# A two-layer four-group mixer on one core: gated outputs of groups C and B wait in DRAM, group D's second keys are made ahead of B's gate, and the ordering clock charges other instructions

## The chip, the cores and the metric

One core of one Trainium2 chip runs the whole program in one launch. The metric is the device time of an execution in microseconds (us). TensorE is called PE, VectorE DVE, ScalarE ACT, GpSimd POOL and SyncE SP, as in the profile; PEld is TensorE's weight load.

## What is computed

Two layers (`DEPTH = 2`), each on 1024 tokens of width 1024, float32. Cut to what matters here:

```python
h = rmsnorm(x, g_pre) @ w_in            # one projection of 3488 columns
ya = swa_sink_attention(a_q, a_k, a_v)  # A: window 128, 4 heads, sinks
yb = short_gated_conv(b_b, b_c, b_x)    # B: b * conv3(c * x)
yc = mla(c_q, c_kv, c_kr)               # C: causal softmax attention, 4 heads
yd = stick_breaking_attention(d_q, d_k, d_v)   # D: 4 heads
y  = rmsnorm(stack([ya, yb, yc, yd])) * silu(gate)   # norm per group of 256
x  = x + rmsnorm(y @ w_out, g_post)
```

Group D's weights for one query block: `a = exp(log_sigmoid(z) + after)`, `after` being a reversed cumulative sum of `log_sigmoid(-z)` over the keys.

## The kernel before

**Precision and tiles.** Every matmul works on operands split into a high and a low part (two reduced-precision tiles per float32 tile), so a projection is three matmuls per 128 rows of the contraction: 24 matmuls for 128 output columns by 512 tokens. One `g` tile holds 128 partitions by 1024 float32 values; the pool `gp` has 34 of them, and they hold the split input (16 tiles, `xt`), queries, keys, values and the groups' outputs `L["y"]` (two tiles a group, one for each half Q of the tokens). Weights come by DMA into two `raw` buffers, are split by ACT (high part) and by POOL or DVE (low part) into three `W` tiles, and from there feed PE.

**The weave.** The program is not written in the order of execution. The class `Weaver` (from line 96) keeps a clock of its own for ACT, DVE, POOL and the DMA queue, and `run` chooses, step by step, among generator functions ("streams"): the first stream in the list whose next operands are there by that clock goes next on PE, or else the one that is ready soonest. The order so found is fixed on every engine (`behind`, `in_order`); at run time each engine takes its instructions in that order and waits where an operand is late. `enter` (from line 255) gives each instruction a duration from its shape; `half` adds 125 ns on ACT and 95 ns on DVE for an output of at most 64 partitions; `pair` keeps DVE and POOL instructions apart that would start inside one another.

**The streams that matter.** `gemm()` (line 1639) issues the projections: C, B, D's values, `d_q(0)`, `d_k(0)`, the gate of group C (`gate(L, 2)`), `d_q(1)`, then half of the gate of group B, then `d_k(1)` (the keys of D's heads 2 and 3), which waits for D's first scores (`need(("scores", l, "D0"))`), then B's other half, A's values and queries, and, after `("scores", l, "D1")`, A's keys. `scores()` issues the score matmuls of C, D heads 0 and 1 (D0), D heads 2 and 3 (D1) and A; it comes ahead of `gemm()` in the list, so projections fill PE where no scores are ready. `pvs()` transposes the weights and multiplies by the values. For D each query block needs, on DVE, a scan and a product over up to 1024 columns. `norms()` normalises each group; B's output has waited in DRAM (`yBd`) since the convolution and is loaded into `g` tiles once `("D", l, 0)` is marked. `z_parts()` splits the gated outputs C, B, D (`z_split`, line 1505) for the output projection after A's scores; `w_out_rows()` loads and splits the output weights; `outs()` does the output projection, eight token tiles by two halves. All DMAs are issued by SP, in one order.

**The tight pool.** When `d_q(1)` is done, the 34 `g` tiles are all taken: 16 of `xt`, 2 each of the outputs B, C and D, 4 of D's values, 6 of D0's queries and keys, 2 of D1's queries. D1's keys need 4 (`room(4)` in `d_k`).

Of the kernel before, what the change touches and what calls it, by code (L numbers as in the profile page):

```python
# [21 lines left out]
P = 128  # L22
# [71 lines left out]
class Weaver:  # L94
# [7 lines left out]
    def __init__(self, tc):  # L102
        self.tc = tc
        self.now = 0.0
        self.busy = {k: [] for k in "AVGDH"}
        self.acc = {}
        self.touched = {}
        self.opened = {}
        self.slots = {}
        self.banks = set()  # L110
        self.read = {}
        self.table = None
        self.users = []
        self.load_at = 0.0
        self.start = 0.0
        self.gone = set()
        self.last, self.tag = {}, {}
        self.funcs = [(0.0, 0)]
        self.port = {"V": [], "G": []}
        self.done = set()  # L120

    def alloc(self, ap, tag, bufs):
# [43 lines left out]
    def after(self, key, a, kinds):  # L166

        p0, p1, lo, hi = self.area(a)
        name = a.tensor.name
        t = self.opened.get(name, 0.0)  # L170
        if name not in self.acc:
            t = max(t, self.last.get(self.tag.get(name), 0.0))
        for (q0, q1, l, h, kind, k), end in self.acc.get(name, {}).items():
            if kind in kinds and q0 < p1 and p0 < q1 and l < hi and lo < h:
                t = max(t, end + LAT.get(k + key, 0.0))
        return t

    def ready(self, key, aps):
        return max([self.after(key, a, "w") for a in aps], default=0.0)
# [68 lines left out]
    def enter(self, key, op, args, kw):  # L248
        aps = [a for a in list(args) + list(kw.values()) if isinstance(a, bass.AP)]
        out = aps[0]  # L250
        outs = [out]
        if "accum_out" in kw:
            outs.append(kw["accum_out"])
        if op == "tensor_tensor_reduce":
            outs.append(aps[-1])
        n = 1
        for d in (aps[1] if op == "tensor_reduce" else out).shape[1:]:
            n *= d
        t = max(self.ready(key, aps[1:]), max(self.after(key, a, "rw") for a in outs))
        read = [a.tensor.name for a in aps[1:] if a.tensor.name in self.banks]  # L260
        bank = bool(read)
        for nm in read:
            for k, end in self.read.get(nm, {}).items():
                t = max(t, end + (LAT[k + key] if k != key else 0.0))
        scalars = sum(
            isinstance(args[i], bass.AP) for i in SCALARS.get(op, ()) if i < len(args)
        )
        func = args[2] if op == "activation" else None
        pair = False
        half = out.shape[0] <= 64 and n >= 128  # L270
        if key == "A":
            dur = (52.0 if bank else 93.0) + 0.833 * n
            dur += 93.5 * sum(isinstance(kw.get(k), bass.AP) for k in ("scale", "bias", "accum_out"))
            dur += 125.0 * half
            if func in TABLES and func:
                t = max(t, self.load_at)
        elif key == "V":
            fast = op == "tensor_scalar" and not bank
            dur = 69.0 + (0.52 if fast else 1.04) * n + 62.0 * scalars + 95.0 * half
            pair = (fast or op == "tensor_tensor") and not bank and n >= 128  # L280
            if op == "tensor_tensor_scan":
                dur = 110.0 + 2.12 * n
                pair = True
            elif op == "tensor_reduce":
                dur += 117.0
        elif op == "affine_select":
            dur = 244.0
        elif op == "memset":
            dur = 36.0 + 0.83 * n
        elif op == "tensor_scalar":  # L290
            dur = 244.0 + 0.833 * n
        else:
            dur = 148.0 + 2.25 * n
            pair = n >= 128
            if args[-1] == ALU.pow:
                dur = 400.0 + 162.0 * n
                pair = False
        t = self.place(key, t, dur, pair=pair)
        if key == "A" and func in TABLES and func:
            self.funcs = self.funcs[-60:] + [(t, func)]  # L300
        self.tc.cur_priority = int(t)
        for nm in read:
            self.read.setdefault(nm, {})[key] = t + dur
        by = "S" if op in ("tensor_tensor_scan", "tensor_tensor_reduce") else key
        for a in outs:
            self.note(by, a, "w", t + dur, t)
        for a in aps[1:]:
            self.note(key, a, "r", t + dur)
        return t
# [78 lines left out]
def tile_hybrid_trunk(  # L388
# [317 lines left out]
    def w_tiles():  # L706

        res = []

        def chunk(L, key, c0, n, spill=False):  # L710
            L["W", key] = []
            per = 512 // n
            for i, k0 in enumerate(range(0, NK, per)):
                kk = min(per, NK - k0)
                src = L["w"][k0 * P : (k0 + kk) * P, c0 : c0 + n]
                res.append((L, key, i, src.rearrange("(k p) c -> p k c", p=P), kk, n, spill))

        for L in LS:
            l = L["l"]
            chunk(L, "C", O_C, 416, True)  # L720
            L["W", "U"], L["W", "KV"] = [], []

            for k in range(2):
                src = mla_w_uq[l, k * P : (k + 1) * P, :].rearrange("p (h d) -> p h d", h=4)
                res.append((L, "U", k, (src[:, :, 0:64], src[:, :, 64:96]), 1, 384, None))
            src = mla_w_ukv[l].rearrange("p (h d) -> p h d", h=4)
            res.append((L, "KV", 0, (src[:, :, 0:64], src[:, :, 64:128]), 1, 512, None))
            for m in range(2):
                for key, c0 in (("c", O_BC), ("x", O_BX), ("b", O_BB)):
                    chunk(L, f"B{key}{m}", c0 + m * P, P)  # L730
            chunk(L, "DV", O_DV, 256, True)
            for key in (
                "DQ0", "DK0", "G20", "G21", "DQ1", "G10", "DK1", "G11", "AV0", "AQ0", "AK0", "AQ1",
                "G30", "G31", "G00", "G01",
            ):
                if key[0] == "G":
                    c0 = O_G + 256 * int(key[1])
                else:
                    c0 = dict(DQ=O_DQ, DK=O_DK, AK=O_AK, AV=O_AV, AQ=O_AQ)[key[:2]]
                chunk(L, key, c0 + int(key[2]) * P, P, key == "G01")  # L740
        return res
# [411 lines left out]


    def group_b(L):
        l, yd = L["l"], L["yBd"]
        for m in range(2):
            us = [ftile(516), ftile(516)]

# [35 lines left out]
        A.activation(dst, pb, AF.Tanh, scale=0.5)  # L1195
        V.scalar_tensor_tensor(dst, dst, 1.0, pb, ALU.add, ALU.mult)

    def gate(L, grp, ms=(0, 1)):
        def ev(Q, pb):
            t = ftile()  # L1200
            silu(t, pb)
            z = L["y"][grp][Q]
            G.tensor_tensor(z[:, m, :], z[:, m, :], t, ALU.mult)
            W.release(t)

        for m in ms:
            yield from chunk_T(L, f"G{grp}{m}", ev)

    def gate_by_half(L):
# [293 lines left out]
    ZORDER = (4, 5, 2, 3, 6, 7, 0, 1)  # L1503

    def z_split(L, grp, Q, wait=True):
        z = L["y"][grp][Q]
        free = W.idle_from("V")
        ts = []
        for m in range(2):
            if wait:  # L1510
                yield lambda: (ts or W.room("g", 2, 34)) and max(0.0, free() - 4000.0)
            ts = ts or [gtile([P, 2, 512]) for _ in range(2)]
            t = ts[m]
            split(t[:, 0, :], t[:, 1, :], z[:, m, :])
# [66 lines left out]
    for l in range(depth):  # L1581
        LS.append(
            dict(
                l=l, w=w_in[l], last=l == depth - 1, tasks=[], y=[[None, None] for _ in range(4)],
                yBd=[dp.tile([P, 2, 512], F32, name=nm("yBd")) for _ in range(NQ)],
                xt=[None, None], zt=[[None] * NK for _ in range(NQ)],
                wo=[[None] * NK for _ in range(2)],
                ss=cp.tile([P, 4 * NT], F32, name=nm("ss")),
# [54 lines left out]
    def gemm():  # L1643
        for L in LS:
# [11 lines left out]
            yield need(("norm", l, 2, 1))  # L1656
            yield from gate(L, 2)
            yield from d_q(L, 1)
            yield need(("norm", l, 1, 1))
            yield from gate(L, 1, (0,))  # L1660
            yield need(("scores", l, "D0"))
            yield from d_k(L, 1)
            W.mark("D", l, 1)
            yield from gate(L, 1, (1,))
            yield from a_v(L)
            yield from a_q(L, 0)
            yield need(("scores", l, "D1"))
            yield from a_k(L)
            yield from a_q(L, 1)
            yield need(("pv", l, "D1", 1))  # L1670
            L["y"][0] = [gtile([P, 2, 512], F32) for _ in range(NQ)]
            W.mark("A", l)
            yield need(("norm", l, 3, 1))
# [123 lines left out]
    def norms():  # L1797
        for L in LS:
            l = L["l"]
            yield need(("B", l))  # L1800
            for Q in range(NQ):
                y = [ftile(), L["yB1"][Q]]
                dma(y[0], L["yBd"][Q][:, 0, :])
                yield W.when(y[0])
                yield from group_norm_cols(l, 1, y)
                for m in range(2):
                    dma(L["yBd"][Q][:, m, :], y[m])
                W.release(*y)
            for Q in range(NQ):
                yield from norm(L, 2, "C", Q)  # L1810
            yield need(("D", l, 0))
            for Q in range(NQ):
                yield room(1)
                L["y"][1][Q] = gtile([P, 2, 512], F32)
                dma(L["y"][1][Q], L["yBd"][Q])
                W.mark("norm", l, 1, Q)
            yield need(("scores", l, "D1"))
            for Q in range(NQ):
# [52 lines left out]
```

## Time and profile before

| | us |
|---|---|
| median of 3 runs | 1160.34 (1159.23 to 1161.73) |
| the profiled execution | 1160.64 |
| its span, first to last instruction | 1158.8 |
| PE busy | 1133.3 (98%) |
| DVE busy | 815.0 (70%) |
| ACT busy | 639.7 (55%) |
| POOL busy | 345.0 (30%) |
| moved by DMA | 71.97 MB, mean 62 GB/s |

The table is to be read against the span. PE has 25.5 us in which no matmul runs, and every other engine has far more; the transfers take about a fifth of the DMA engines' time. The span has these stages, the same in both layers: C and B projections with C's attention (to 250 us in the first layer), D (250 to 393), A (393 to 490), output (490 to 570).

### The profile page before, as it was taken

To read this page: it belongs to the slowest core of one execution; us is meant where nothing else is said; L and a number is where in the kernel's file an instruction comes from. 1 tells how busy PE (TensorE), PEld (TensorE's weight loads), DVE (VectorE), ACT (ScalarE), POOL (GpSimd) and SP (SyncE) were. 2 spreads that over 40 slices of the span, in tenths; PEclk is the share of its full clock that TensorE was granted. 3 is DMA by queue.
4 is the path that set the end of the run, shared out by engine and by line. 5 is a ranking of instruction groups with operands and counts; after the bars stand their busy time and mean duration, and the time that the engine had idled before them with its cause. 6 is when DMAs were issued, how large, how long until landed. Compare 5 with 4: busy or idle time off the path is not lost. (4 is left out here: it accounts for less than half of the span.)

```text
span 1158.8 us, 17859 instructions
## 1 busy us (share of the span) xinstructions
PE 1133.3 (98%) x6302; PEld 978.0 (84%) x6302; DVE 815.0 (70%) x1682; ACT 639.7 (55%) x1443; POOL 345.0 (30%) x480
## 2 busy tenths in 40 slices
PE   8999999999999999999999999999999999999997
PEld 6988889988888788878889888899888787887886
DVE  6868788549868988842764677874697789887324
ACT  7666566246656667632554655652664566875211
POOL 3215144114324244210231352530342333531000
PEclk9999999999999999999999999999999999999999
DMA  6120312121011012311450121121201101114123
GB/s 224 42 64 29 83 26 58 46 74 37 19 46 28 19 38 72 107 46 62 150 173 20 38 68 42 38 64 38 82 19 38 37 19 37 29 55 164 55 77 123
DMA packets 72677, 71.97 MB, mean 62 GB/s; under 512 B 10062, under 2 KB 59276, under 8 KB 72588
## 3 DMA queue, kind: packets, MB, share of 16 engines
q1 hardware_dynamic: 72588, 70.83, 20.6%
q8 instruction: 50, 0.82, 0.3%
q14 instruction: 39, 0.32, 0.1%
HBM read 55.09 MB, written 11.53 MB: 57 GB/s over the span
## 5 line engine op out<-in xcount | busy, mean ns | idle before, releaser
L497 PE MATMUL xw<-xg,xw 128*128 128x512 f32 x2064 | 516.8, 396 | 3.5 <-DVE xf L85 2.7
L497 PEld LDWEIGHTS xw<-xg,xw 128*128 128x128 f32 x2064 | 376.4, 188 | 78.1 <-DVE xf L85 4.4
L497 PE MATMUL xsc<-xg,xg 128*128 128x512 f32 (+7 forms) x1400 | 304.4, 363 | 0.4 <-DVE xs L85 0.4
L497 PEld LDWEIGHTS xsc<-xg,xg 128*128 128x128 f32 (+1 forms) x1400 | 238.9, 190 | 35.4 <-DVE xs L85 1.6
L85 POOL TENSOR_SCALAR xP<-xP,xs 128x256 f32<-128x256 f32 (+7 forms) x128 | 81.9, 652 | 169.7 <-DVE xs L85 77.7
L85 ACT CAST xPT<-xtr 128x512 fp32r<-128x512 f32 (+1 forms) x192 | 100.5, 553 | 56.4 <-PE xtr L501 54.9
L501 PE MATMUL xtr<-ident,xP 128*128 128x128 f32 (+1 forms) x843 | 122.5, 273 | 5.6 <-DVE xP L85 4.9
L85 DVE TENSOR_TENSOR xPT<-xtr,xPT 128x512 fp32r<-128x512 f32 (+1 forms) x192 | 116.3, 629 | 13.1 <-ACT xPT L85 12.6
L497 PE MATMUL xw<-xg,xg 128*128 128x416 f32 (+2 forms) x648 | 116.8, 327 | 0.2 <-DVE xg L85 0.2
L497 PE MATMUL xpv<-xPT,xg 128*128 128x256 f32 (+1 forms) x720 | 114.9, 286 | 0.4 <-DVE xPT L85 0.3
L497 PEld LDWEIGHTS xpv<-xPT,xg 128*128 128x128 f32 x720 | 102.9, 189 | 10.6 <-DVE xPT L85 1.9
L501 PEld LDWEIGHTS xtr<-ident,xP 128*128 128x128 f32 (+1 forms) x843 | 97.4, 140 | 16.0 <-DVE xP L85 6.7
L85 POOL TENSOR_TENSOR xw<-xraw,xw 128x512 fp32r<-128x512 f32 x47 | 68.4, 1458 | 138.9 <-ACT xw L85 106.5
L85 DVE TENSOR_TENSOR xg<-xw,xg 64x512 fp32r<-64x512 f32 (+1 forms) x112 | 62.8, 573 | 62.4 <-ACT xg L85 61.2
L85 ACT CAST xg<-xw 64x512 fp32r<-64x512 f32 (+1 forms) x112 | 53.6, 493 | 93.2 <-PE xw L497 81.6
L85 ACT ACTIVATE xP<-xP,xs 128x256 f32<-128x256 f32 (+7 forms) x128 | 80.7, 631 | 43.7 <-DVE xs L85 40.3
L497 PEld LDWEIGHTS xw<-xg,xg 128*128 128x128 f32 x648 | 102.1, 189 | 2.7 <-DVE xg L85 0.4
L85 DVE TENSOR_TENSOR_SCAN xP<-xP 128x128 f32<-128x128 f32 (+3 forms) x64 | 90.5, 1414 | 3.0 <-ACT xP L85 2.7
L85 POOL TENSOR_TENSOR xt<-xt 64x128 f32<-64x128 f32 x64 | 41.6, 650 | 146.5 <-DVE xt L85 131.6
L85 ACT ACTIVATE xP<-xsc 128x512 f32<-128x512 f32 (+2 forms) x192 | 79.7, 514 | 6.6 <-DVE xP L85 6.0
L85 ACT ACTIVATE xt<-xsc 128x512 f32<-128x512 f32 x32 | 19.1, 598 | 113.2 <-PE xsc L497 89.3
L85 ACT COPY xt<-xpv 64x512 f32<-64x512 f32 x80 | 46.7, 584 | 53.5 <-PE xpv L497 52.4
(129 smaller groups left out, 1284.5 us busy)
## 6 DMA issues: line engine op xcount, KB each, us to landing
xraw<-in_w_in_dram SPq DMA_DIRECT2D x96, 256.0 KB, 2.8
xP<-in_w_out_dram SPq DMA_DIRECT2D x16, 512.0 KB, 4.3
xg<-in_x_dram SPq DMA_DIRECT2D x8, 512.0 KB, 8.6
xg<-xP SPq DMA_DIRECT2D x32, 128.0 KB, 2.4
xP<-in_x_dram SPq DMA_DIRECT2D x8, 512.0 KB, 4.1
xP<-xs SPq DMA_DIRECT2D x8, 512.0 KB, 3.8
xs<-xP SPq DMA_DIRECT2D x7, 512.0 KB, 3.6
out_dram<-xP SPq DMA_DIRECT2D x7, 512.0 KB, 2.6
```

What stands on the lines that cost most here:

```text
L85: ins = real(*args, **kw)
L497: in_order(T.matmul(ps, lhs, rhs, start=start, stop=stop, skip_group_check=True))
L501: in_order(T.transpose(ps, src, idn))
```

## The change

Outputs of C and B: the gate writes each gated tile to a DRAM buffer `yd` (2 groups x 2 halves x 512 KB a layer) and gives its `g` tile back; `z_split` loads it again (512 KB) before it splits it, and the split waits for the load by the clock. `d_k(1)` moves ahead of the whole of B's gate, does not wait for D's first scores any more, and B's output is loaded only once D1's keys are made. A's output tiles wait for room in the pool and not for D's last product. The order of weight loads follows. In the clock, `half` becomes `held`: the extra time is charged to an instruction on an engine whose operands begin at another 32-partition row than those of the engine's last instruction; `pair` now covers every DVE instruction of 128 or more columns that reads no PSUM, `memset` apart, and POOL's `tensor_scalar`.

```diff
+    def held(self, key, out, ins):
+        res = False
+        for kind, aps in (("r", ins), ("w", [out])):
+            for a in aps:
+                k = key, kind, a.tensor.name in self.banks
+                p0 = self.area(a)[0] // 32
+                res = res or self.rows.get(k, p0) != p0
+        for kind, aps in (("r", ins), ("w", [out])):
+            for a in aps:
+                self.rows[key, kind, a.tensor.name in self.banks] = self.area(a)[0] // 32
+        return res
...
-        half = out.shape[0] <= 64 and n >= 128
+        half = self.held(key, out, aps[1:])
...
-            pair = (fast or op == "tensor_tensor") and not bank and n >= 128
+            pair = not bank and n >= 128 and op != "memset"
...
         elif op == "tensor_scalar":
             dur = 244.0 + 0.833 * n
+            pair = n >= 128
...
-                "DQ0", "DK0", "G20", "G21", "DQ1", "G10", "DK1", "G11", "AV0", "AQ0", "AK0", "AQ1",
+                "DQ0", "DK0", "G20", "G21", "DQ1", "DK1", "G10", "G11", "AV0", "AQ0", "AK0", "AQ1",
...
-    def gate(L, grp, ms=(0, 1)):
+    def gate(L, grp):
+
         def ev(Q, pb):
             t = ftile()
             silu(t, pb)
             z = L["y"][grp][Q]
             G.tensor_tensor(z[:, m, :], z[:, m, :], t, ALU.mult)
             W.release(t)
+            if m and grp in L["yd"]:
+                dma(L["yd"][grp][Q], z)
+                W.release(z)
...
     def z_split(L, grp, Q, wait=True):
-        z = L["y"][grp][Q]
         free = W.idle_from("V")
         ts = []
+        back = grp in L["yd"]
+        if back:
+            yield room(3)
+            L["y"][grp][Q] = gtile([P, 2, 512], F32)
+            dma(L["y"][grp][Q], L["yd"][grp][Q])
+        z = L["y"][grp][Q]
         for m in range(2):
             if wait:
-                yield lambda: (ts or W.room("g", 2, 34)) and max(0.0, free() - 4000.0)
+                yield lambda: (ts or W.room("g", 2, 34)) and max(
+                    0.0, free() - 4000.0, W.ready("A", [z]) if back else 0.0
+                )
...
             yield from gate(L, 2)
             yield from d_q(L, 1)
-            yield need(("norm", l, 1, 1))
-            yield from gate(L, 1, (0,))
-            yield need(("scores", l, "D0"))
             yield from d_k(L, 1)
             W.mark("D", l, 1)
-            yield from gate(L, 1, (1,))
+            yield need(("norm", l, 1, 1))
+            yield from gate(L, 1)
...
-            yield need(("pv", l, "D1", 1))
+            yield room(2)
             L["y"][0] = [gtile([P, 2, 512], F32) for _ in range(NQ)]
...
-            yield need(("D", l, 0))
+            yield need(("D", l, 1))
             for Q in range(NQ):
                 yield room(1)
                 L["y"][1][Q] = gtile([P, 2, 512], F32)
-                dma(L["y"][1][Q], L["yBd"][Q])
+                dma(L["y"][1][Q], L["yd"][1][Q])
```

## Rows read from the trace of the kernel before

**Rows 1.** page, part 1: busy us, share of span, instructions by engine.

```profile
PE 1133.3 (98%) x6302; PEld 978.0 (84%) x6302; DVE 815.0 (70%) x1682; ACT 639.7 (55%) x1443; POOL 345.0 (30%) x480
```

**Rows 2.** waits of PE: waited for, us in total, times, longest us.

```profile
PE xtr L501 <- DVE xP L85: 4.9, 3, 2.3
...
PE xtr L501 <- DVE xt L85: 3.7, 2, 2.2
...
PE xw L497 <- DVE xf L85: 2.7, 4, 0.9
```

**Rows 3.** timeline of PE: start, duration, instructions, idle before and its releaser.

```profile
310.10 0.23 PE L497 MATMUL xsc<-maskD,identb 128*128 128x128 bf16 x1
...
333.63 0.34 PE L497 MATMUL xsc<-xg,xg 128*128 128x128 f32 x2
...
356.32 0.98 PE L497 MATMUL xw<-xg,xw 128*128 128x512 f32 x3 [0.46 <-DVE xf L85]
...
391.39 0.98 PE L501 MATMUL xtr<-ident,xP 128*128 128x128 f32 x7 [2.32 <-DVE xP L85]
...
392.72 5.07 PE L497 MATMUL xw<-xg,xw 128*128 128x512 f32 x21
...
960.97 0.98 PE L501 MATMUL xtr<-ident,xP 128*128 128x128 f32 x7 [2.33 <-DVE xP L85]
```

**Rows 4.** windows: length; busy PE, PEld, DVE, ACT, POOL; clock; DMA.

```profile
310.10:333.60 23.50, 23.50 (x123) 20.10 (x123) 14.99 (x22) 9.73 (x18) 5.48 (x7) 1.00 0.09 23
...
333.60:392.70 59.10, 55.95 (x309) 45.66 (x308) 50.30 (x64) 39.91 (x87) 21.24 (x19) 1.00 0.14 36
```

**Rows 5.** the same view of the projection matmuls' tile xw alone.

```profile
250.00:310.10 60.10, 39.57 (x157) 28.47 (x157) 9.52 (x15) 11.28 (x19) 8.20 (x6) 1.00 0.15 36
...
310.10:333.60 23.50, 20.03 (x84) 15.43 (x84) 5.38 (x8) 5.17 (x9) 0.76 (x1) 1.00 0.09 23
...
333.60:392.70 59.10, 36.77 (x145) 26.16 (x145) 7.53 (x12) 11.30 (x19) 10.93 (x7) 1.00 0.14 36
```

**Rows 6.** timeline of DVE: the 1023-column product of group D, twice.

```profile
298.46 1.23 DVE L85 TENSOR_TENSOR xP<-xP,xP 128x1023 f32<-128x1023 f32 x1
...
389.30 2.03 DVE L85 TENSOR_TENSOR xP<-xP,xP 128x1023 f32<-128x1023 f32 x1
```

**Rows 7.** timeline of POOL: a weight split.

```profile
388.71 1.54 POOL L85 TENSOR_TENSOR xw<-xraw,xw 128x512 fp32r<-128x512 f32 x1 [3.12 <-ACT xw L85]
```

**Rows 8.** DMA issues: count, KB each, median us to landing.

```profile
xP<-in_w_out_dram SPq DMA_DIRECT2D x16, 512.0 KB, 4.3
...
xg<-xyBd SPq DMA_DIRECT2D x4, 512.0 KB, 4.2
```

**Rows 9.** timeline of PE where the output stage of each layer begins.

```profile
495.37 0.66 PE L501 MATMUL xtr<-ident,xt 128*128 128x128 f32 x4 [1.50 <-DVE xt L85]
...
495.78 2.98 PE L497 MATMUL xsc<-xg,xg 128*128 128x512 f32 x12
...
1060.54 2.90 PE L497 MATMUL xsc<-xg,xg 128*128 128x512 f32 x12
...
1065.61 1.11 PE L501 MATMUL xtr<-ident,xt 128*128 128x128 f32 x4 [2.17 <-DVE xt L85]
...
1066.38 4.26 PE L497 MATMUL xsc<-xg,xg 128*128 128x512 f32 x12
```

**Rows 10.** timeline of ACT ahead of the second of these.

```profile
1032.35 1.13 ACT L85 CAST xg<-xg 128x512 fp32r<-128x512 f32 x2
...
1062.22 0.62 ACT L85 CAST xw<-xP 128x512 fp32r<-128x512 f32 x1 [2.91 <-DMA xP<-in_w_out_dram]
...
1062.87 0.58 ACT L85 COPY xt<-xpv 64x512 f32<-64x512 f32 x1
```

**Rows 11.** windows: columns as in Rows 4, the granted clock after that stall.

```profile
1065.60:1069.00 3.40, 3.39 (x10) 2.90 (x11) 2.81 (x5) 1.39 (x3) 2.29 (x2) 0.51 0.47 154
```

**Rows 12.** chain that ended last: start, duration, what.

```profile
1055.11 7.09 DMA xP<-in_w_out_dram
```

More of the change, by code (lines that the diff above doesn't have):

```diff
@@ L119, in __init__ @@
         self.port = {"V": [], "G": []}
+        self.rows = {}
         self.done = set()
@@ L1155, in group_b @@
     def group_b(L):
-        l, yd = L["l"], L["yBd"]
+        l, yd = L["l"], L["yd"][1]
         for m in range(2):
@@ L1204, in ev @@
             W.release(t)
-        for m in ms:
+            if m and grp in L["yd"]:
+                dma(L["yd"][grp][Q], z)
+                W.release(z)
+        for m in range(2):
             yield from chunk_T(L, f"G{grp}{m}", ev)
@@ L1584, in tile_hybrid_trunk @@
                 l=l, w=w_in[l], last=l == depth - 1, tasks=[], y=[[None, None] for _ in range(4)],
-                yBd=[dp.tile([P, 2, 512], F32, name=nm("yBd")) for _ in range(NQ)],
+                yd={g: [dp.tile([P, 2, 512], F32, name=nm("yd")) for _ in range(NQ)] for g in (1, 2)},
                 xt=[None, None], zt=[[None] * NK for _ in range(NQ)],
@@ L1802, in norms @@
                 y = [ftile(), L["yB1"][Q]]
-                dma(y[0], L["yBd"][Q][:, 0, :])
+                dma(y[0], L["yd"][1][Q][:, 0, :])
                 yield W.when(y[0])
@@ L1806, in norms @@
                 for m in range(2):
-                    dma(L["yBd"][Q][:, m, :], y[m])
+                    dma(L["yd"][1][Q][:, m, :], y[m])
                 W.release(*y)
```

## The prediction

> **What bounds the kernel now.** I first read the busy table: PE is busy 98% of the span, and no other engine comes above 70% [rows 1]. All matmuls stay, so the change can win only from the 25 us in which PE stands idle, and can lose by adding to them. The waits of PE come next: they show where that idle time sits and which engine ends it. The largest is PE's wait for DVE's product `xP`, ahead of a transpose, 4.9 us in three waits; then 3.7 us in two for `xt`, and 2.7 us in four for `xf`, the gate [rows 2]. The timeline of PE puts places to these. Of the first, two are 2.32 and 2.33 us long, at 391.39 and 960.97, the end of D1's scores in either layer [rows 3]. The wait for `xt` is 1.50 us in the first layer and 2.17 us in the second, where the output stage has just begun and A's last norm is late [rows 9]. These three sources are 11.3 of the 25 us; I looked for the change's effect there.
>
> Why PE idles at 391 is seen from what follows. D1's last score is out soon after, and the next thing is 21 projection matmuls, A's keys, which were not to start before D1's scores were done [rows 3]. So at 391 PE had no projection left to fill with: it waited for one DVE product. In the hole ahead, the reverse: D0's last score matmul ends at 310.1, D1's first starts at 333.63 [rows 3], and in between 84 of PE's 123 instructions are projections [rows 4, 5]. DVE is busy 14.99 of 23.5 us in that hole, but 50.30 of 59.1 us while D1's scores run [rows 4]. Filler is spent while DVE has nothing of D to do, and is missing 60 us later.
>
> **The change part by part.** *D1's keys first.* The projections before and after are the same 384 matmuls. By 310.1, 157 of them show in the trace [rows 5], that is C's gate (96), `d_q(1)` (48) and the start of the next chunk. With the keys as the next chunk, some 35 of their 48 are left at 310.1; at 20.03/84 = 0.24 us each [rows 5] that is 8.4 us, with D0's last products among them, 23.5 - 20.0 = 3.5 us. D1's scores would begin near 322 to 325 and not at 333.6, and end as much sooner, about 10 us. During D1 the old order used 145 projections [rows 5]; the new one has 192 ahead of A's keys (B's gate 96, A's values 48, a query chunk 48), so some 45 remain when D1's scores end. The planned idle at 391 then goes. A part of it was not planned: the product that PE waits for took 2.03 us, the same shape elsewhere 1.23 [rows 6], and a POOL weight split had begun 0.59 us before it [rows 7]. That 0.8 us can stay, if filler is laid by a clock that did not see it. The gain lies between 2.3 - 0.8 = 1.5 and 2.3 us a layer; which split meets which product is chance, so I take the middle, 1.9.
>
> *B's gate inside D1.* Its first half ran in the hole with no stall; its second half cost a 0.46 us wait at 356.32 for the gate's bank, inside D1 [rows 3]. Now both halves lie there: between 0 and 0.46 us a layer more, a gain being excluded because PE was busy for 23.50 of 23.50 us in the hole [rows 4]. I take 0.3, nearer to the row that shows it.
>
> *The parking.* A layer gains four stores and four loads of 512 KB; the two loads of B's ungated output were there and only move. A load like these lands in 4.2 us [rows 8]. The stores of C are queued on SP behind POOL's product, with weight loads behind them; up to five weight tiles (two `raw`, three `W`) are ahead of PE, 24 matmuls or 5.5 us each, so I cost this at nothing; without that cover it would cost the product's delay once, 1 to 2 us. D1's keys reuse the freed tiles 48 projections (11 us) after the store was issued, and B's load has the same 11 us against 4.2. The loads before `z_split` are followed on ACT by the split itself, in order; behind it stand the evacuation of A's products and the gate's tanh. Those splits began at 1032.35 [rows 10] and the output matmuls at 1060.54 [rows 9]: 28 us for four loads that could take 4 x 4.2 = 17 us one after the other, and the tile pool has places free (C and B no longer hold four). Price: 0, up to another stall as large as the one that is there (below).
>
> *The other clock and the looser wait for A's output tiles.* No instruction is added. They can move any small wait: bounded by one such wait, 0.46 us a layer either way. I take 0.
>
> Sum: 2 x (-1.9 + 0.3) = -3.2 us against the profiled execution's 1160.64, that is 1157.4. The median lies 0.3 below that execution, so **1157.1**. By the bounds alone (-2.3 to -1.04, and 0.46 either way, a layer) the likeliest case runs from 1154.8 to 1159.2. What is late next is the layer's end, as before.
>
> **The rivals.** *The layer's end gets a second late load (slower).* At 1062.22 ACT had sat 2.91 us waiting for an output-weight load, and the copy of A's last product, 1062.87, stood behind it [rows 10]. [...] The program's chain of work holds that load: 7.09 us from issue to landing [rows 12], where the median of its kind is 4.3 [rows 8]. A reload that arrives with these, or splits pushed into the end, would hold the same queue. [...] It decides when the last reload is still out at about 1055, or its split stands ahead of A's last copy. For it: ACT's order is fixed by a clock that is already late there. Against: the DMA engines are little used until then, and the pool is looser.
>
> [...]
>
> *POOL and DVE collide more.* The row is the 2.03 us product against 1.23, begun 0.59 us after POOL [rows 6, 7]. POOL's 5.48 us of work in the hole stands beside a DVE that is idle a third of the time [rows 4]; in the change it stands inside D, in seven instructions. If PE pays 0.8 us for two of them a layer, 3.2 us go back: 1160.3. [...] Against a large size: D1's stretch has 19 POOL instructions [rows 4] and two PE waits above 0.4 us [rows 3].
>
> *The keys don't come earlier.* After C's tiles are freed, `xt` 16, D's output 2, D's values 4, D0's queries and keys 6, D1's queries 2 make 30; D1's keys need 4: exactly 34. If one tile more is held at that point, `d_k(1)` waits for D0's scores as before and the hole stays: 1160.3.
>
> **How the numbers follow.** Forecast 0.48; collisions 0.10; keys not earlier 0.10; hold gone 0.14; second late load 0.18. About 0.2% (2.3 us) is what a measurement of this kernel can tell from no change, so faster means under 1158.0 and slower over 1162.7. Faster: 0.8 of the forecast's 0.48 and the 0.14, 0.52. Slower: 0.15 of the last rival's 0.18. Same: the rest, 0.33. The range reaches down to the hold gone and up to the middle of the late load's 1162.5 to 1166.4: 1151.5 to 1164.0, with some 0.15 left out.
>
> **What would show it.** Right: D1's first score near 323 and its last near 383; no PE wait of over 1 us there; a projection chunk still running after D1's last score; the hole's DVE share up from 64% to over 80%. The parking is right if no PE wait ends on a tile read back, and if ACT's splits of C and B don't wait for DMA by more than a microsecond. Wrong: D1's scores still start after 330 (keys not earlier); waits at the gates or transposes of D1 adding up to 2 us (collisions); a wait at the output stage over 2.2 us, or a second stretch of half clock (late load).

## The result and the profile after

The changed kernel takes **1148.97 us** (median of 4 executions, 1148.41 to 1149.37); the kernel before, on the same chip, 1160.69 us. The ratio is 0.990, with a 95% interval of 0.9882 to 0.9917: some 11.7 us, or 1.0%, faster. The forecast was 3.2 us faster, and the time lies 2.5 us below the low end of its range. The sign was right and the size was not.

The page's busy table of after, to be read against [rows 1]:

```profile
span 1147.3 us, 17932 instructions
...
PE 1130.7 (99%) x6302; PEld 978.8 (85%) x6302; DVE 810.8 (71%) x1688; ACT 638.6 (56%) x1443; POOL 336.4 (29%) x474
```

PE has the same 6302 instructions and is idle for 1147.3 - 1130.7 = 16.6 us, where it was idle for 25.5. Its busy time fell by 2.6 us as well, part of it the stretch of half clock of [rows 11] (0.51), which has no counterpart at the layer's end here. The profiled execution of after has its clock at 0.50 elsewhere: at the program's start, from 10.7 to 14.1 us, behind a wait of 1.10 us; and at 0.51 in the last 3.4 us of the span, in which no matmul runs. The waits of PE in after (waited for, us in total, times, longest):

```profile
PE xtr L594 <- DVE idle L85: 2.7, 1, 2.7
...
PE xw L513 <- DVE xf L85: 1.6, 2, 0.8
PE xw L513 <- ACT xg L85: 1.1, 1, 1.1
...
PE xtr L517 <- DVE xt L85: 0.7, 2, 0.3
...
PE xtr L517 <- DVE xP L85: 0.3, 1, 0.3
```

Against [rows 2]: `xP` from 4.9 to 0.3, `xt` from 3.7 to 0.7, the gate `xf` from 2.7 in four waits to 1.6 in two. The largest wait left, 2.7 us, is the program's first and stood in the kernel before too. PE's timeline at D1's scores (start, duration, instructions, idle before and its releaser), to be read against [rows 3]:

```profile
310.54 0.23 PE L513 MATMUL xsc<-maskD,identb 128*128 128x128 bf16 x1
310.58 2.98 PE L513 MATMUL xw<-xg,xw 128*128 128x512 f32 x12
...
320.59 0.34 PE L513 MATMUL xsc<-xg,xg 128*128 128x128 f32 x2
...
340.14 0.51 PE L513 MATMUL xpv<-xPT,xg 128*128 128x256 f32 x2 [0.27 <-DVE xPT L85]
...
381.70 0.23 PE L513 MATMUL xsc<-maskD,identb 128*128 128x128 bf16 x1
381.74 2.98 PE L513 MATMUL xw<-xg,xw 128*128 128x512 f32 x12
```

D1's first score stands at 320.59 and no longer at 333.63, its last at 381.70 and no longer at 392.7; projections run on behind it, and the only wait inside is 0.27 us. The windows of the old hole, now 10.0 us, and of D1's stretch (columns as in [rows 4]), and then the hole for the projection matmuls' tile `xw` alone:

```profile
310.60:320.60 10.00, 10.00 (x54) 8.49 (x54) 9.69 (x13) 5.92 (x11) 1.23 (x2) 1.00 0.03 3
320.60:381.80 61.20, 60.93 (x352) 51.49 (x350) 54.21 (x73) 40.28 (x89) 23.59 (x22) 1.00 0.22 69
```

```profile
310.60:320.60 10.00, 8.70 (x36) 6.50 (x36) 3.42 (x5) 2.96 (x5) 0.00 (x0) 1.00 0.03 3
```

DVE's share of the hole went from 14.99 of 23.50 us to 9.69 of 10.00, and the projections in it from 84 to 36: that is where the idle time beside the filler was. The second place is the layer's end, to be read against [rows 9]:

```profile
476.47 0.79 PE L513 MATMUL xpv<-xPT,xg 128*128 128x256 f32 x6
477.10 5.68 PE L513 MATMUL xw<-xg,xw 128*128 128x512 f32 x24
483.13 0.66 PE L517 MATMUL xtr<-ident,xt 128*128 128x128 f32 x4 [0.34 <-DVE xt L85]
483.54 2.98 PE L513 MATMUL xw<-xg,xg 128*128 128x512 f32 x12
486.36 2.88 PE L513 MATMUL xw<-xg,xw 128*128 128x512 f32 x12
489.08 0.84 PE L513 MATMUL xsc<-xg,xg 128*128 128x512 f32 x3
```

Behind A's last product (`xpv`, 476.47) 48 projections (24, 12 and 12) still stand; in the kernel before only 3 did. They cover A's last norm, whose transposes wait 0.34 us here, in place of 1.50 and 2.17.

Where the 11.5 us of PE's span went, by the starts of matmuls in the two profiled executions:

| Stretch | before, layer 1 / 2 | after, layer 1 / 2 | difference |
|---|---|---|---|
| D0's first score to A's first score | 171.90 / 171.89 | 169.07 / 169.10 | -2.83 / -2.79 |
| A's first score to the 25th output matmul | 77.42 / 79.13 | 75.26 / 75.23 | -2.16 / -3.90 |
| all the rest (start, other groups, tails) | | | +0.21 |

So the attention of D gave 5.6 us and the layer's end 6.1.

### The profile page after: what moved, and what is told of

It reads as the page before. It is cut to its first block, busy times and chain, and to the rows that moved or that the text cites. A ratio compares the mean times of both kernels' runs of the same rounds, so it can differ in the third digit from the quotient of the medians.

```text
span 1147.3 us, 17932 instructions
## 1 busy us (share of the span) xinstructions
PE 1130.7 (99%) x6302; PEld 978.8 (85%) x6302; DVE 810.8 (71%) x1688; ACT 638.6 (56%) x1443; POOL 336.4 (29%) x474
## 4 chain that ended last, share of the span: by engine, by line
PE 84%; DVE 8%; ACT 4%; issue 2%; POOL 1%; DMA 1%; SPq 0%; DVEq 0%; POOLq 0%; ACTq 0%
PE xw L513 43%; PE xsc L513 24%; PE xtr L517 9%; PE xpv L513 7%; DVE xP L85 4%; ACT xP L85 2%; DVE xg L85 1%; ACT xg L85 1%; DVE xt L85 1%; DVE xPT L85 1%; DMA xg<-in_w_in_dram 1%; DVE xs L85 1%; ACT xt L85 0%; POOL xs L85 0%; POOL xP L85 0%
## 5 line engine op out<-in xcount | busy, mean ns | idle before, releaser
L85 DVE TENSOR_TENSOR_SCAN xP<-xP 128x128 f32<-128x128 f32 (+3 forms) x64 | 93.8, 1466 | 1.7 <-ACT xP L85 1.2
L85 POOL TENSOR_TENSOR xw<-xraw,xw 128x512 fp32r<-128x512 f32 x37 | 52.1, 1409 | 121.1 <-ACT xw L85 118.8
## 6 DMA issues: line engine op xcount, KB each, us to landing
xg<-in_x_dram SPq DMA_DIRECT2D x8, 512.0 KB, 10.7
```

Of the source, the lines that this page charges most:

```text
L85: ins = real(*args, **kw)
```

## The experiments

**D's order alone undone.** `keys_late` is the changed kernel with the old projection order; parking, clock and tile wait stay.

```diff
-                "DQ0", "DK0", "G20", "G21", "DQ1", "DK1", "G10", "G11", ...
+                "DQ0", "DK0", "G20", "G21", "DQ1", "G10", "DK1", "G11", ...
...
             yield from d_q(L, 1)
+            yield need(("norm", l, 1, 1))
+            yield from gate(L, 1, (0,))
+            yield need(("scores", l, "D0"))
             yield from d_k(L, 1)
             W.mark("D", l, 1)
-            yield need(("norm", l, 1, 1))
-            yield from gate(L, 1)
+            yield from gate(L, 1, (1,))
...
-            yield need(("D", l, 1))
+            yield need(("D", l, 0))
```

> The changed kernel (parking, new clock) with the old order of projections: first half of B's gate, then D1's keys after D0's last score, then the other half. If the earlier keys carry D's gain, D takes 171.9 us again from D0's first score to A's first score, the 2.3 us wait at the end of D1 is back and 2.8 us a layer are lost, 5.6 in all; the gain at A's end shows whether it hangs on the earlier D1: with it 1154.6 (parking or clock carry A's end), without it 1160.7 (the earlier D1 carries all).

Measured: 1154.46 us, ratio 0.9947 (0.9928 to 0.9967). PE's timeline shows D's wait as it was, and no wait at the layer's end:

```profile
390.80 0.98 PE L517 MATMUL xtr<-ident,xP 128*128 128x128 f32 x7 [2.32 <-DVE xP L85]
...
486.81 0.60 PE L517 MATMUL xtr<-ident,xt 128*128 128x128 f32 x4
```

From D0's first score to A's takes 171.97 and 172.03 us, as before. So the order of the keys is worth 1154.46 - 1148.97 = 5.5 us (5.8 against `no_clock`, on the same chip), which is the first row of the table within 0.2 us, and the layer's end does not hang on it: with the old order it is free too.

**The clock alone, in and out.** `clock_only` is the kernel before with the two new lines of the clock; `no_clock` is the changed kernel with the old ones.

```diff
-        half = out.shape[0] <= 64 and n >= 128
+        half = self.held(key, out, aps[1:])
...
-            pair = (fast or op == "tensor_tensor") and not bank and n >= 128
+            pair = not bank and n >= 128 and op != "memset"
...
         elif op == "tensor_scalar":
             dur = 244.0 + 0.833 * n
+            pair = n >= 128
```

> The kernel before with the new ordering clock alone (held in place of half, the wider pair); nothing is parked and D1's keys stay where they were. Two theories on the 6.1 us that the changed kernel gains between A's first scores and the output stage (2.16 in the first layer, 3.90 in the second). Clock theory: the new order frees A's last products from what holds them, so this kernel gains about 6 us, to about 1154.6, and its PE waits of 1.50 and 2.17 us at the output stage are gone, while the 2.32 us wait at the end of D1 stays. Structure theory: the gain needs the parked tiles or the earlier D1, so this kernel stays within 1 us of 1160.7 and keeps all four waits.

> The changed kernel with the old ordering clock. Clock theory: D's gain of 2.8 us a layer stays, the gain at A's end goes: about 1155, with waits of 1.5 to 2.2 us at the output stage. Structure theory: about 1149, as the changed kernel, with no wait above 0.9 us after the start.

Measured: `clock_only` 1156.89 us, ratio 0.9962 (0.9947 to 0.9976). D's 2.33 us waits stay; the waits at the output stage are gone, with 9 projections behind A's last product. `no_clock` 1148.69 us, ratio 0.9897 (0.9875 to 0.9919), the same as the changed kernel. The clock alone wins some 4.8 us by the medians, and it does so by freeing the layer's end, which the new order and the parking free without the clock. In the changed kernel it is worth nothing in sum. Within D it costs a little: from D0's first score to A's takes 168.61 and 168.67 us in `no_clock`, 169.07 and 169.10 in the changed kernel.

The looser wait for A's output tiles changes nothing: the changed kernel with the old wait in its place gives the same program, so there is no run of it.

**The layer's end, three ways.** [Rows 10] say that ACT had the copy of A's last product queued behind an output-weight split which waited for its load. `late_wout` is the kernel before, with its clock told that the loads of the second half of the output weights land 3 us later; nothing else changes. `park_only` has the parking (and the looser wait) alone, with the order and the clock of before. `spread` has only the splits of C's and B's outputs held 3 us each in the plan.

```diff
-        dma(raw, w_out[L["l"], k * P : (k + 2) * P, c].rearrange("(k p) c -> p k c", p=P))
+        dma(raw, w_out[L["l"], k * P : (k + 2) * P, c].rearrange("(k p) c -> p k c", p=P), 3000.0 * hf)
...
-        self.note("D", out, "w", t + dur, issue)
+        self.note("D", out, "w", t + dur + late, issue)
```

> The kernel before, its clock told that loads of the second half of the output weights land 3 us later than it reckons, so that their splits are ordered later; nothing else. If ACT's wait for such a load (2.25 and 2.91 us), with the copy of A's last product behind it, is what makes PE wait 1.50 and 2.17 us at the output stage, these waits and the half clock after the second go: 1.5 + 2.17 + 1.73 = 5.4 us, about 1155.3. If A's last product is late for another reason (ACT and DVE too full with splits in A's last products), the waits stay above 1 us and the time stays within 1.5 us of 1160.7.

Measured: 1157.04 us, ratio 0.9963 (0.995 to 0.9977). ACT's timeline in the kernel before (first layer), and then in `late_wout`:

```profile
491.98 0.62 ACT L85 CAST xw<-xP 128x512 fp32r<-128x512 f32 x1 [2.25 <-DMA xP<-in_w_out_dram]
492.62 0.58 ACT L85 COPY xt<-xpv 64x512 f32<-64x512 f32 x1
```

```profile
490.63 0.62 ACT L85 CAST xg<-xP 128x512 fp32r<-128x512 f32 x1
491.91 0.58 ACT L85 COPY xt<-xpv 64x512 f32<-64x512 f32 x1 [0.66 <-PE xpv L497]
```

In `late_wout` the copy stands ahead of the split and waits for PE alone; the transposes of A's last norm (495.20) then follow with no wait, though still only 3 projections stand behind A's last product. So the order of two copies on ACT was the cause in the kernel before.

In park_only:

```diff
+            if m and grp in L["yd"]:
+                dma(L["yd"][grp][Q], z)
+                W.release(z)
...
+        back = grp in L["yd"]
+        if back:
+            yield room(3)
+            L["y"][grp][Q] = gtile([P, 2, 512], F32)
+            dma(L["y"][grp][Q], L["yd"][grp][Q])
```

> The kernel before with the parking alone: C's and B's gated outputs wait in DRAM, but D1's keys stay behind D0's scores and the clock is the old one. In its fixed order 21 projections follow A's last product (3 in the kernel before, 48 in the changed kernel). Parking theory (the reloads spread the splits of C and B, so ACT and DVE are free for A's products, which then end ahead of the last projections): the waits of 1.50 and 2.17 us at the output stage and the half clock behind the second are gone, D's wait of 2.3 us stays, about 1155. Theory that only the earlier D1 moves A's end: both kinds of wait stay, about 1160.5.

Measured: 1158.09 us (1154.66 to 1159.46), ratio 0.9968 (0.9956 to 0.998). D's waits of 2.31 and 2.32 us stay, the waits for `xt` are gone, with 21 projections behind A's last product.

In spread:

```diff
         free = W.idle_from("V")
         ts = []
+        if wait and grp != 3:
+            began = W.now
+            yield lambda: began + 3000.0
```

> The kernel before with one thing more: the splits of C's and B's gated outputs are each held back by 3 us in the planned order, as a reload would, with no DMA. Its order has 27 projections behind A's last product. If it is the spreading of these splits, and not the tiles' room or the DMA, that lets A's products end early, the output stage's waits go and D's stay: about 1155 to 1156. If room in the pool is needed, or the earlier D1, it stays at 1160 to 1161.

Measured: 1158.61 us, ratio 0.9976 (0.9963 to 0.9989). The waits for `xt` are gone (27 projections are left there), and a new one of 1.56 us stands at 940.45. All three, `clock_only` and `keys_late` lost the hold, by edits of different kinds. Where it is gone, the number of projections behind A's last product runs from 3 (`late_wout`) to 51 (`no_clock`), and in all five the stretch from A's first score to the 25th output matmul takes 75.06 to 75.65 us, close to the changed kernel's 75.26 and 75.23. By the medians `clock_only`, `late_wout`, `park_only` and `spread` gain 3.4 to 4.8 us and not the 6.1 of the table, `keys_late` 7.2. The granted clock, whose mean differs from execution to execution (0.995 to 0.999 in 17 of the kernel before), has a part in this: in the profiled execution of the kernel before it fell to 0.51 behind the hold [rows 11], where the four transposes and twelve matmuls of [rows 9] took (1.11 - 0.66) + (4.26 - 2.98) = 1.73 us more than in the first layer, 1.73 of the 6.1, and it fell behind no wait of D; in those of `clock_only`, `late_wout` and `park_only` it fell behind D's wait in both layers, in that of `keys_late` behind none (last section).

**D alone, with less parking.** `early_back` has D1's keys early, the old clock, B's output not parked, and C's brought back as soon as D0's tiles are free, behind B's load, and not just ahead of its split.

```diff
-            if m and grp in L["yd"]:
+            if m and grp == 2:
                 dma(L["yd"][grp][Q], z)
                 W.release(z)
...
                 W.mark("norm", l, 1, Q)
+            for Q in range(NQ):
+                yield room(1)
+                L["y"][2][Q] = gtile([P, 2, 512], F32)
+                dma(L["y"][2][Q], L["yd"][2][Q])
+            W.mark("back", l)
```

> The old clock, D1's keys early, but only C is parked, and only until D1's keys are made and D0's tiles are free again; at A's end nothing is reloaded, as in the kernel before. Theory that the parking at A's end carries the gain there: D gains 2.8 us a layer, A's end keeps a wait of over 1 us in each layer, about 1155. Theory that the earlier D1 suffices: its fixed order has 18 projections behind A's last product, the waits at the output stage go, about 1149.5.

Measured: 1146.66 us (1146.35 to 1146.8), ratio 0.9877 (0.9862 to 0.9892). The same kernel again, beside the changed kernel and beside a version of itself with the new clock:

> The version with D1's keys early, only C parked and only through D, the old clock, again, beside the changed kernel on the same chip. If its lead of 2.3 us over the changed kernel is real: 0.9875 to 0.988 of the kernel before, no PE wait above 0.9 us, and D0's first score to the 25th output matmul in 243.1 us against 244.3 in the changed kernel. If it was chance of the chip or of the start, both come out within 1 us of one another.

> The changed kernel again, as a partner for the version above: about 0.990 of the kernel before if the first measurement holds.

> The version above with the new ordering clock. Theory that the new clock is worth nothing once the structure has removed the long waits: within 1 us of the version above. Theory that the changed kernel is slower than that version by the new clock's order and not by the reloads: slower by 1 to 2 us. If the reloads are what costs, it equals the version above and both lead the changed kernel by about 2 us.

| Kernel | median us | ratio (95%) |
|---|---|---|
| `early_again` | 1146.66 | 0.9878 (0.9862 to 0.9894) |
| `early_clock` | 1147.10 | 0.9883 (0.9864 to 0.9902) |
| `after_again` | 1148.69 | 0.9894 (0.9878 to 0.991) |

The executions of `early_again` (1146.41 to 1147.10) all lie below those of `after_again` (1148.10 to 1149.02): this version beats both kernels. PE's timeline shows the waits that it has left ahead of A in the first layer, both ahead of D1 and both there before:

```profile
281.95 0.96 PE L512 MATMUL xw<-xg,xw 128*128 128x512 f32 x3 [0.89 <-DVE xf L85]
...
302.58 2.32 PE L512 MATMUL xw<-xg,xw 128*128 128x512 f32 x9 [0.38 <-DVE xg L85]
```

The earlier keys, with C's parking alone, take both D's wait and the end's away. The new clock gives nothing here either (0.4 us the other way); the other 1148.69 - 1147.10 = 1.6 us between this version and the changed kernel are the parking of B and the late reloads. Of these, 1.3 lie behind A's first score: from there to the 25th output matmul `after_again` takes 75.35 us in either layer, `early_clock` 74.70 and 74.69. The changed kernel has four small waits of PE from 310 to 484 us (0.27, 0.23, 0.21 and 0.34 us, 1.05 in all) where `early_again` has none listed. The first two come with the new clock, for `early_clock` has them and `no_clock` hasn't; whether the parking makes the other two is not shown.

**The clock of PE.** `warm` is the kernel before with matmuls on zeros, whose result nothing reads, where PE idles: at D1's end and ahead of A's last norm.

```diff
+            yield from warm(("scores", l, "D1"))
             yield need(("scores", l, "D1"))
...
+        for i in range(extra):
+            in_order(T.matmul(pb, idle[:, 0:P], idle, start=True, stop=True, skip_group_check=True))
```

> The kernel before with matmuls of zeros, whose result nobody reads, put into PE's two longest waits of each layer: 8 where the projections run out at D1's end, 8 ahead of the transposes of A's last norm. No useful work moves. PE's waits still last, filled. If a wait costs only its own length, the median stays at that of the kernel before, about 1161, and single times spread as widely. If PE's idle stretch also lets the granted clock fall to its lower level in some executions (3.4 us at 0.5, worth 1.6 to 1.7 us each), the median falls to that of the kernel before's fastest runs, 1157 to 1158.5, and its times lie closer together.

Measured: 1160.43 us (1159.17 to 1161.73), ratio 0.999 (0.9979 to 1.0). The timeline at D1's end:

```profile
390.08 1.46 PE L1650 MATMUL xw<-idle 128*128 128x512 bf16 x6
...
392.45 0.98 PE L501 MATMUL xtr<-ident,xP 128*128 128x128 f32 x7 [0.80 <-DVE xP L85]
```

The plan itself put 6 zero matmuls there and one behind them, 1.5 us of work: most of the 2.32 us was idle that the plan knew of, and what it didn't know is the 0.80. The single times lie within 2.6 us where those of the kernel before beside it have 6.2, and the only matmuls at half clock in the profiled execution stand at its start (from 10.7: seven projections take 2.80 us, and 1.59 in the kernel before); but the median didn't fall as expected. The hold is still there in this run: ACT waits 2.41 us for the load in the second layer, with the copy behind the split, and the zero matmuls only fill PE's wait. On the size of the clock's part this run is inconclusive; the rows of the other kernels show it (below).

**POOL's splits given to DVE.** `early_dve` is `early_back` with the low parts of six weight chunks (C's and B's gates, D1's queries and keys) made by DVE alone. It was meant to keep POOL's splits away from D's products; those of A's weights, which also fall into D, may still go to POOL.

```diff
-            W.sooner((G, V), m, raw, t).tensor_tensor(
+            own = key in ("G20", "G21", "DQ1", "DK1", "G10", "G11")
+            (V if own else W.sooner((G, V), m, raw, t)).tensor_tensor(
```

> The version above with the low parts of the weights of C's gate, B's gate and D1's queries and keys made on DVE alone, not on POOL or DVE by choice. If the remaining PE waits of 0.89 us at the gate and 0.38 us stand behind DVE products that a POOL weight split holds up (2.03 us against 1.23 for the same shape), they go and 1 to 2.5 us are won in the two layers; if DVE's own load is what makes it late, 14 splits of 0.6 us more on DVE lengthen these waits and the time grows by 1 us or more.

Measured: 1165.17 us, ratio 1.0033 (1.0022 to 1.0044), so 18.5 us slower than `early_back`. PE's waits, its timeline, and a window with its clock (columns as in [rows 4]):

```profile
PE xw L512 <- DVE xf L85: 7.8, 4, 3.0
PE xw L512 <- DVE xg L85: 6.4, 4, 2.8
```

```profile
321.24 2.32 PE L512 MATMUL xw<-xg,xw 128*128 128x512 f32 x9 [2.84 <-DVE xg L85]
...
368.38 4.21 PE L512 MATMUL xw<-xg,xw 128*128 128x512 f32 x9 [3.02 <-DVE xf L85]
```

```profile
371.20:374.60 3.40, 3.40 (x15) 3.11 (x14) 0.00 (x0) 0.42 (x1) 0.00 (x0) 0.50 0.00 0
```

DVE makes 57 weight splits of this kind in place of 43, POOL 31 in place of 45. Fourteen splits of 0.73 us more on DVE, and PE waits up to 3 us for DVE's evacuations, with the clock at 0.50 from 367.8 to 374.6. All of the loss lies in D: 177.78 and 179.00 us from D0's first score to A's, in place of 168.66 and 168.63 in `early_again`. But the run did not do what it was meant to. DVE's timeline in it:

```profile
365.97 1.77 DVE L85 TENSOR_TENSOR xP<-xP,xP 128x767 f32<-128x767 f32 x1
...
386.00 2.06 DVE L85 TENSOR_TENSOR xP<-xP,xP 128x1023 f32<-128x1023 f32 x1
```

Three products of D1's stretch in each layer are lengthened like these two beside a POOL split, where `early_again` has none there (the two shapes take 0.96 and 1.23 us undisturbed). So the run says nothing on what D without collisions is worth, and the 3.02 us wait stands behind one of them. What it shows is that giving POOL's work to DVE cost 18.5 us here, far more than the 0.8 us that a collision takes.

## Why the prediction was wrong in size

**D1's keys first: right place, term too small.** The forecast had the first score near 322 to 325, the last near 383 and some 45 projections left over; the rows say 320.6, 381.7, and projections running on behind it (some 36, by the windows of `xw`). Priced at -1.9 a layer, and -1.6 net of the gate, it measured -2.83 and -2.79 (-3.28 and -3.23 in `no_clock`, without the new clock). Two steps failed. I kept back up to 0.8 us for a collision that the plan hadn't seen. `warm` shows that 0.8 us were indeed unplanned. But in the new order that collision doesn't happen, nor any other in D1's stretch. A product of DVE that was lengthened in the kernel before, and then the timelines of DVE and of POOL in after:

```profile
384.51 2.02 DVE L85 TENSOR_TENSOR xP<-xP,xP 128x895 f32<-128x895 f32 x1
```

```profile
371.18 1.23 DVE L85 TENSOR_TENSOR xP<-xP,xP 128x1023 f32<-128x1023 f32 x1
...
382.16 1.09 DVE L85 TENSOR_TENSOR xP<-xP,xP 128x895 f32<-128x895 f32 x1
...
386.62 1.20 DVE L85 TENSOR_TENSOR xP<-xP,xP 128x1023 f32<-128x1023 f32 x1
```

```profile
371.27 2.29 POOL L85 TENSOR_TENSOR xw<-xraw,xw 128x512 fp32r<-128x512 f32 x1 [2.35 <-ACT xw L85]
```

With the old order of keys, four products of D1's stretch in each layer start while a POOL split runs and are lengthened (in the first layer of the kernel before those of 511, 639, 895 and 1023 columns: 1.53, 1.67, 2.02 and 2.03 us, in place of 0.69, 0.82, 1.09 and 1.23), some 3.4 us of DVE's time. That is so in the kernel before and in all six runs with the old order. With the keys early none of D1's is, `early_dve` apart; where the two still meet, at 371.2, DVE began first and POOL's split took 2.29 us, where their median is 1.3. The prediction counted one such product, and as a rival had PE pay 0.8 us for two more of them a layer. How much of D's gain is the projections' cover and how much the collisions' going, no run takes apart. And B's gate inside D1 was priced at +0.3 with a gain excluded: its 0.46 us wait at 356.32 is gone, and so are two smaller ones (0.21 and 0.17 us, at 370.98 and 387.05). D1's stretch had 2.32 + 0.46 + 0.21 + 0.17 = 3.16 us of waits and has 0.27, and 0.23 behind it.

A price was missing too: behind D's wait the clock fell to 0.50 in some executions (7 of 12 such waits, last section). It did not in the profiled one of before, so I saw no row of it; in `clock_only` it did.

**The layer's end "as before": wrong.** This step carried 0 us and measured -2.16 and -3.90, half of the result. I had the mechanism, the order of two copies on ACT with a late load ahead of one, and gave its going, as a rival on top of the forecast, a chance of 0.14 and 1157.1 - 5.4 = 1151.7 us, the 5.4 being the waits of 1.50 and 2.17 us and the 1.73 worked out above from [rows 9]. The chance was low because nothing in the change aims there. That reason was the error. The hold hung on a coincidence: a split planned just ahead of a copy, a load later than planned, and only 3 projections left to cover it. Six edits that moved the plan removed it (`clock_only`, `late_wout`, `park_only`, `spread`, `keys_late`, `early_back`); only `warm`, which adds nothing but zero matmuls, kept it. What had to be asked was what keeps the coincidence alive under a new order, and I knew of nothing. My own count pointed the same way: with some 45 projections left over at D1's end, more than 3 could be expected behind A's last product, and there are 48 (with the same keys, 18 in `early_back`). With the two terms as measured the sum is -5.6 - 6.1 = -11.7, the measured gain. My range ended at the hold-gone rival's single value, with no spread of D's term under it.

**The parking: nearly as priced.** It was put at 0, and no wait of PE or ACT in after ends on a tile read back. The page's DMA issues of after (KB each, us to landing), to be read against [rows 8]:

```profile
xg<-xyd SPq DMA_DIRECT2D x12, 512.0 KB, 5.1
...
xyd<-xg SPq DMA_DIRECT2D x8, 512.0 KB, 3.0
```

A reload takes 5.1 us where 4.2 stood, and has the room for it. Still, B's parking and the late reloads cost some 1.6 us, 0.8 a layer, as `early_clock` beside `after_again` shows; the forecast had nothing between 0 and another large stall.

**The other clock and the tile wait: right at 0 in sum** in the changed kernel (`no_clock`, `early_clock`); by the medians it is 0.3 us slower with the new clock.

**The other rivals.** Second late load: fell; ACT's splits come after the copy and wait for no load. Its 1162.5 to 1166.4 us put 5.4 to 9.3 on the forecast, up to a wait of 2.91 us and 1.73 of low clock in each layer: no run shows that cost, and what the runs showed at that place is a gain of 2.16 and 3.90 us. ACT's timeline in after:

```profile
477.30 0.58 ACT L85 COPY xt<-xpv 64x512 f32<-64x512 f32 x1
477.78 0.63 ACT L85 ACTIVATE xt<-xg 128x512 f32<-128x512 f32 x1
...
479.27 1.66 ACT L85 CAST xg<-xP 128x512 fp32r<-128x512 f32 x3
```

Collisions in D: fell, by D1's waits of 0.27 us, and went the other way: 14 of D's products are lengthened in the profiled execution of before, by 0.58 to 0.92 us, and 6 in that of after, 4 of them by 0.85 to 0.92 and 2 by 0.19. Keys not earlier: fell, by the start at 320.6; the tiles were enough.

## What to carry to other kernels

Move filler to where the engine that ends the waits is full, and away from where it idles: here 36 projections run in the hole while DVE is at 97%, where 84 ran beside a DVE at 64%, and D gained 5.6 us. In a fixed, planned order, price each stall that rests on a near tie (a split one place ahead of a copy, three instructions of cover) as likely to go under a new plan (six of seven edits here), and let it add to the forecast. And park or reload only what frees the tile that is short: the same gain came with half the traffic, and 2 us more.

## What the runs showed of the hardware

Behind a wait of 2.31 to 2.33 us in an otherwise full PE stream the granted clock fell to 0.50 in some executions and stayed at 1.00 in others. The windows behind D's wait, in the kernel before and in `clock_only` (columns as in [rows 4]):

```profile
391.60:395.00 3.40, 3.40 (x20) 2.73 (x19) 3.32 (x5) 3.40 (x7) 1.21 (x1) 1.00 0.27 74
```

```profile
391.60:395.00 3.40, 3.40 (x12) 2.49 (x11) 3.32 (x5) 2.87 (x7) 1.55 (x1) 0.50 0.19 56
```

The wait ahead was 2.32 and 2.33 us; in the second the clock is at 0.50, and 12 instructions are in the window in place of 20. From D0's first score to A's first takes 171.9 to 172.0 us where it doesn't fall (both layers of before and of `keys_late`) and 173.4 to 173.6 where it does (both layers of `clock_only` and `park_only`): a fall costs some 1.4 to 1.7 us beside the wait itself. In the profiled executions of the kernel before, `clock_only`, `late_wout`, `keys_late`, `park_only` and `spread` it fell behind 7 of the 12 such waits. The time of the kernel before goes with its mean granted clock: in 17 executions beside `after_again` it runs from 1158.6 us at 0.999 to 1163.8 at 0.995. The changed kernel, with no wait over 1 us behind its start, stays within 1.0 us in each of two sets of four. The spread was narrower in `warm` too, where such waits are filled: 2.6 us in place of 6.2. That these falls make the whole spread is not shown, for the executions without a profile don't tell where it fell; why the clock falls in one execution and not in the next is open.
